# The last MLP product of a two-layer trunk: where the right half of the second token half is accumulated in PSUM

## The chip, the cores and the metric

The kernel runs on one core of a Trainium2 chip. The metric is the device time of one execution in microseconds. Before the change three runs gave 563.83, 564.20 and 564.38 us, so the median is 564.2 us.

## The reference

Two layers work on 256 tokens of width 1024. Each is a token mixer (block attention in layer 0, dilated windows in layer 1), a LayerNorm, an MLP and a second LayerNorm. Only the MLP and the norm behind it matter here:

```python
def layer_norm(x, g, b):
    mu = mean(x); var = mean((x - mu) ** 2)
    return (x - mu) * rsqrt(var + 1e-5) * g + b

def sq_relu_mlp(x, w_in, w_out):               # w_in 1024 x 4096, w_out 4096 x 1024
    return jnp.square(jax.nn.relu(x @ w_in)) @ w_out

h = layer_norm(DEEPNORM_ALPHA * h + sq_relu_mlp(h, w_in, w_out), ln_mlp_g, ln_mlp_b)
```

The norm at the end of layer 1 gives the output.

## The kernel before, in words

**Precision.** Every operand is kept as two rounded parts, hi and lo, and every product is three: hi by hi, hi by lo and lo by hi. All of these are recorded by one helper, `mm` (line 353), so nearly every TensorE row carries this line, and the tiles' names tell products apart. A weight tile of 128 x 1024 is loaded into `raw` by SyncE's queue; ScalarE rounds it to `whi` (line 344) and VectorE subtracts to get `wlo` (line 349).

**The MLP (`Mlp.rest`, from line 877).** The 4096 hidden columns are cut into eight chunks of 512. Chunk 0 is done ahead, in another form. For each chunk from 1 to 7 the first product (`mm_wstat_wide`, line 472) forms four tiles of 128 hidden columns by 256 tokens, each in a PSUM bank with the tag `tp`: per tile eight matmuls of 512 columns (hi weights by hi and lo inputs side by side) and eight of 256 (lo weights). `relu_sq_T` (line 833) takes a bank out: ScalarE copies one half (line 838), VectorE adds the other (line 535), squares (line 542), ScalarE and VectorE split the result into `ahi` and `alo`. One chunk behind, `do_out` (line 886) issues the second product with the four slices of 128 hidden columns of the chunk before, called k-tiles here; there are 32, numbered 0 to 31.

**The second product (`mm_rows`, line 515).** The 256 tokens are two halves of 128 (m = 0 and m = 1), and the outputs are 1024 columns wide. A *piece* is a PSUM bank with the first column and the number of columns that it collects. For each k-tile and each token half, every piece gets three matmuls. `new_acc` (line 814) lists the pieces: normally two of 512 columns for each token half, in four banks of the tag `acc`. In the last MLP (`last=True`, layer 1) the right half of m = 1 is two pieces of 256 columns: one in its `acc` bank and one in a bank taken from the four `tp` banks. That `tp` bank is held from k-tile 0 to the end of the kernel, so three are left for the first product's tiles. Per k-tile m = 1 then costs 3 matmuls of 512 columns and 6 of 256, where m = 0 costs 6 of 512.

**The tail (`out_and_ln`, line 820).** `TAIL` (line 30) says how many of the last k-tiles are kept back for each sub-layer; its last entry, 8, is for the last MLP. With them the pieces are finished one by one, and not k-tile by k-tile, so that VectorE can take out the first pieces while TensorE works on the next.

**The norm (`ln_half`, line 765).** For each piece VectorE computes `ALPHA * z + acc` into the token tile (lines 776 and 542) and statistics by `bn_stats` (line 779); `step` is the smallest piece, so 512 for m = 0 and 256 for m = 1 of the last MLP. Then `bn_aggr` (line 782), an addition (line 783), a power on GpSimd (line 785), two multiplications per half (line 542) and the output DMAs (line 798).

**The order of instructions.** The lists above are not the order on the engines. Each operation is recorded with an estimated cost, and a planner (`Plan.order`, line 159) simulates the engines with these costs, gives each operation a due time and picks the most urgent ready one. Buffers of a tag are given out in the order of their making; the tag `tp` alone may be taken out of turn if a bank is spare. So a change in costs or in banks held can change the order on every engine.

Of the kernel before, what the change touches and what calls it, by code (L numbers as in the profile page):

```python
# [10 lines left out]
ALU = mybir.AluOpType  # L11

P = 128
S = 256
# [8 lines left out]
ALPHA = (2.0 * DEPTH) ** 0.25  # L23
# [3 lines left out]
BIG = 3.0e38  # L27
NCH = DFF // 512
NX = (1, 1)
TAIL = (6, 4, 6, 8)  # L30
NSLOT = 10

GROUPS = ((0, 1, 2, 3),)
# [251 lines left out]
def tile_trunk(  # L285
# [37 lines left out]
    def mk(shape, dt, tag, bufs, space=None):  # L323
        uid[0] += 1
        return plan.buf(Bufs(space or sb, bufs), shape, dt, tag, bufs, f"{tag}_{uid[0]}")

    def psum(tag):
        return mk([P, 512], F32, tag, 4, ps_pool)
# [7 lines left out]
    def dve(n, aps=0, fast=False):  # L336
        return n / (1920 if fast else 960) + 0.07 + 0.06 * aps
# [14 lines left out]
    def mm(out_ap, lhsT, rhs, start, stop):  # L352
        nc.tensor.matmul(out_ap, lhsT, rhs, start=start, stop=stop)  # L353
# [160 lines left out]

    def mm_rows(pieces, item, m):
        (ahi, alo, j), w, pos, total = item
        first, last = pos == 0, pos == total - 1
        t = slice(m * P, (m + 1) * P)

        def go():  # L520
            a, b = ahi.t[:, j, t], alo.t[:, j, t]
            for acc, c0, n in pieces:
                mm(acc.t[:, :n], a, w.hi.t[:, c0 : c0 + n], first, False)
                mm(acc.t[:, :n], a, w.lo.t[:, c0 : c0 + n], False, False)
            for acc, c0, n in pieces:
                mm(acc.t[:, :n], b, w.hi.t[:, c0 : c0 + n], False, last)

        op(
            "PE", 3 * sum(n / 2400 + 0.0135 for _, _, n in pieces), go,
            [(w.hi, 0), (w.lo, 0), (ahi, (j, m)), (alo, (j, m))], [acc for acc, _, _ in pieces],  # L530
        )

    def tt(n, out_ap, a, b, alu, r, w, eng="DVE", extra=0.0):
        if eng == "DVE":
            op("DVE", dve(n) + extra, lambda: nc.vector.tensor_tensor(out_ap(), a(), b(), op=alu), r, w)  # L535
        else:
            op("POOL", n / 480 + 0.17, lambda: nc.gpsimd.tensor_tensor(out_ap(), a(), b(), op=alu), r, w)

    def stt(n, aps, dst, a, s, b, o0, o1, r, w):
        op(  # L540
            "DVE", dve(n, aps),
            lambda: nc.vector.scalar_tensor_tensor(dst(), a(), s(), b(), op0=o0, op1=o1), r, w,  # L542
        )
# [221 lines left out]
    def ln_half(pieces, m, gb, last, ahead):  # L765
        g, b = gb
        z = xtok[m]
        step = min(n for _, _, n in pieces)
        st = mk([P, 4, 6], F32, "bst", 2)
        mv = mk([P, 2], F32, "mv", 3)  # L770
        rs = mk([P, 2], F32, "rstd", 3)
        prev = []
        ns = D // step
        for acc, c0, n in pieces:
            c = slice(c0, c0 + n)
            stt(n, 0, lambda c=c: z.t[:, c], lambda c=c: z.t[:, c], lambda: ALPHA, lambda acc=acc, n=n: acc.t[:, :n],
                ALU.mult, ALU.add, [(z, c0 // 512), acc] + prev, [(z, c0 // 512)])
            for i in range(c0 // step, (c0 + n) // step):
                op("DVE", dve(step), lambda i=i: nc.vector.bn_stats(st.t[:, i, :], z.t[:, i * step : (i + 1) * step]),  # L779
                   [(z, c0 // 512)], [(st, i)])  # L780
                prev = [(st, i)]
        op("DVE", 0.24, lambda: nc.vector.bn_aggr(mv.t, st.t[:, :ns, :]), [st], [mv])
        op("DVE", 0.07, lambda: nc.vector.tensor_scalar(rs.t[:, 0:1], mv.t[:, 1:2], EPS, None, op0=ALU.add),
           [mv], [(rs, 0)])
        op("POOL", 0.98, lambda: nc.gpsimd.tensor_tensor(rs.t[:, 1:2], rs.t[:, 0:1], expo.t, op=ALU.pow),
           [(rs, 0), expo], [(rs, 1)])
        for n in range(2):
            c = slice(n * 512, (n + 1) * 512)
            stt(512, 1, lambda c=c: z.t[:, c], lambda c=c: z.t[:, c], lambda: mv.t[:, 0:1], lambda c=c: g.t[:, c],
                ALU.subtract, ALU.mult, [(z, n), mv, g], [(z, n)])  # L790
            split_last = last and m == 1 and n == 1
            for i, w in enumerate((256, 256) if split_last else (512,)):
                cw = slice(c.start + 256 * i, c.start + 256 * i + w)
                key = (z, ("part", i) if split_last else n)
                stt(w, 1, lambda cw=cw: z.t[:, cw], lambda cw=cw: z.t[:, cw], lambda: rs.t[:, 1:2],
                    lambda cw=cw: b.t[:, cw], ALU.mult, ALU.add, [(z, n), (rs, 1), b], [key])
                if last:
                    op("SP", ISSUE, lambda cw=cw: nc.sync.dma_start(out[m * P : (m + 1) * P, cw], z.t[:, cw]),
                       [key], (), early=8.0 - 8.0 * m - n)
            if not last:  # L800
                ps = psum("tp")
                transposes(
                    ps, [(j * P, lambda k=n * 4 + j: z.t[:, k * P : (k + 1) * P]) for j in range(4)], [(z, n)],
                    ahead,
                )
                t = slice(m * P, (m + 1) * P)
                keys = [(n * 4 + j, m) for j in range(4)]
                split(
                    512, lambda ps=ps: ps.t.rearrange("p (j s) -> p j s", j=4), lambda n=n: xs[n].t[:, :, 0, t],
                    lambda n=n: xs[n].t[:, :, 1, t], [ps], [(xs[n], (0, *k)) for k in keys],  # L810
                    [(xs[n], (1, *k)) for k in keys],
                )

    def new_acc(last=False):
        acc = [[(psum("acc"), n * 512, 512) for n in range(2)] for _ in range(2)]
        if last:
            acc[1] = [acc[1][0], (acc[1][1][0], 512, 256), (psum("tp"), 768, 256)]
        return acc

    def out_and_ln(acc, items, ntail, gb, last, between):  # L820
        k = len(items) - ntail
        for item in items[:k]:
            for m in range(2):
                mm_rows(acc[m], item, m)
        for m in range(2):
            for piece in acc[m]:
                for item in items[k:]:
                    mm_rows([piece], item, m)
            if m == 1 and between:
                between()  # L830
            ln_half(acc[m], m, gb, last, AHEAD["turn"][m])
# [27 lines left out]
    class Mlp:  # L859
# [17 lines left out]
        def rest(self, between):  # L877
            i, nx, chunks = self.i, self.nx, self.chunks
            self.half(1)
            acc = new_acc(self.last)  # L880
            nkt = DFF // P
            ntail = TAIL[2 * i + 1]
            pend = list(range(nx))
            tail = []

            def do_out(c):
                for j in range(4):
                    pos = c * 4 + j
                    item = ((*chunks[c], j), load_w(wout[i][pos]), pos, nkt)
                    if nkt - pos <= ntail:  # L890
                        tail.append(item)
                    else:
                        for m in range(2):
                            mm_rows(acc[m], item, m)

            for c in range(nx, NCH):
                if c == 4:
                    gb = load_gb(2 * i + 1)
                    if i == 0:
                        ropes.append(const(rope1, [P, 2, S], "ropet"))  # L900
                        late["m1"] = const(mask1, [P, 2, 512], "m1")
                chunks[c] = act_tiles()
                for js in GROUPS:
                    tiles = [(psum("tp"), load_w(win[i][c * 4 + j])) for j in js]
                    mm_wstat_wide(tiles)
                    for (ps, w), j in zip(tiles, js):
                        relu_sq_T(ps, *chunks[c], j)
                pend.append(c)
                while len(pend) > 1:
                    do_out(pend.pop(0))  # L910
            while pend:
                do_out(pend.pop(0))
            out_and_ln(acc, tail, len(tail), gb, self.last, between)

    def layer0(between):
# [84 lines left out]
        items = [((*attn[j // 4], j % 4), load_w(wo0[j]), j, 8) for j in range(8)]  # L1000
        out_and_ln(new_acc(), items, TAIL[0], (late["g"], late["b"]), False, between)

# [16 lines left out]
    def layer1(between):  # L1019
# [72 lines left out]
        items = [((*attn[j // 3], j % 3), load_w(wo1[j]), j, 6) for j in range(6)]  # L1092
        out_and_ln(new_acc(), items, TAIL[2], gb, False, between)

# [116 lines left out]
```

## Time and profile before

| what | value |
|---|---|
| median of three runs | 564.2 us (563.83 to 564.38) |
| the profiled execution's own time | 565.42 us |
| its span in the trace | 563.5 us |
| TensorE matmul (PE) busy in the span | 554.2 us |
| VectorE (DVE) busy | 413.3 us |
| ScalarE (ACT) busy | 300.5 us |
| mean granted TensorE clock | 0.996 |

The span runs from the first to the last event of the trace; the execution's own time is 1.92 us longer. A matmul row gives its start and its modelled duration. Since matmuls are pipelined, the time that one costs in a row of them is the distance from its start to the next start, not its duration. The chain of work that ended last lists, in order of time, stretches of one engine, line and output tile with their number of matmuls; a few per cent of the records may be missing, and what a stretch is called (`acc` or `tp`) is the tag of the bank that is written. Layer 0's MLP lies at about 130 to 293 us, layer 1's at about 376 to 563.5 us.

### The profile page before, as it was taken

The page shows a single profiled execution, that of the slowest core. Times are in us where ns is not written, and L with a number is a line of the kernel's source. Part 1 is how long each engine was busy: PE and PEld are TensorE (multiplying, and loading weights), DVE is VectorE, ACT ScalarE, POOL GpSimd, SP SyncE. Part 2 cuts the span into 40 slices and gives each one's busy share as a digit, 9 for nine tenths or more (in the row PEclk, how much of TensorE's full clock was granted, in tenths as well). Part 3 has the DMA queues.
Part 4 walks back from the last instruction along what each step waited for, and adds up shares of the span by engine and source line. Part 5 has one row for each costly group of instructions (what it writes and reads, how often), then busy time and mean ns, then how long its engine had stood idle before and what let it go on. Part 6 is the DMA issues. An engine that isn't in the chain of part 4 may idle for free.

```text
span 563.5 us, 8714 instructions
## 1 busy us (share of the span) xinstructions
PE 554.2 (98%) x3310; PEld 477.1 (85%) x3310; DVE 413.3 (73%) x727; ACT 300.5 (53%) x491; POOL 8.3 (1%) x13
## 2 busy tenths in 40 slices
PE   8999999999999999999999999999999999999994
PEld 8988877888888888888888889888888888888884
DVE  5799899897764854855879899789856647648554
ACT  5558889168455455455534566546545554544400
POOL 0000000000000000000000000010000000000000
PEclk9999999999999999999999999999999999999998
DMA  8996155638884755656437534516876547553001
GB/s 302 342 360 217 47 187 177 235 106 298 275 274 150 255 158 185 222 158 217 131 130 245 182 120 166 195 66 202 314 238 218 186 153 223 186 188 112 1 1 74
DMA packets 30137, 105.62 MB, mean 187 GB/s; under 512 B 3344, under 2 KB 3984, under 8 KB 30096
## 3 DMA queue, kind: packets, MB, share of 16 engines
q1 hardware_dynamic: 30096, 105.07, 55.4%
q8 instruction: 26, 0.43, 0.3%
q14 instruction: 15, 0.12, 0.1%
HBM read 104.01 MB, written 1.05 MB: 186 GB/s over the span
## 4 chain that ended last, share of the span: by engine, by line
PE 95%; ACT 2%; DVE 1%; DMA 1%; issue 0%; DVEq 0%; SPq 0%; ACTq 0%
PE acc L353 55%; PE tp L353 38%; PE tp L658 3%; ACT whi L344 1%; DMA raw<-in_xw_dram 1%; DVE tok L542 0%; DVE ta L535 0%; ACT pt L666 0%; DVE sc L634 0%; ACT ta L563 0%; ACT q0hi L344 0%; ACT q1hi L344 0%; DVE bst L779 0%; DVEq L1205 0%; SPq L340 0%
## 5 line engine op out<-in xcount | busy, mean ns | idle before, releaser
L349 DVE TENSOR_TENSOR wlo<-raw,whi 128x1024 fp32r<-128x1024 f32 (+3 forms) x186 | 218.4, 1191 | 102.5 <-PE tp L353 50.0
L344 ACT ACTIVATE whi<-raw 128x1024 fp32r<-128x1024 f32 (+1 forms) x184 | 189.1, 1043 | 141.0 <-PE tp L353 69.4
L353 PE MATMUL acc<-whi,ahi 128*128 128x512 f32 (+1 forms) x312 | 119.1, 382 | 0.0
L353 PE MATMUL acc<-wlo,ahi 128*128 128x512 f32 (+1 forms) x312 | 117.4, 380 | 0.0
L353 PE MATMUL tp<-xs,whi 128*128 128x512 f32 x448 | 106.0, 390 | 0.0
L353 PE MATMUL acc<-whi,alo 128*128 128x512 f32 (+1 forms) x312 | 100.8, 379 | 0.0
L353 PEld LDWEIGHTS tp<-xs,whi 128*128 128x128 f32 x448 | 83.5, 188 | 17.0
L353 PEld LDWEIGHTS acc<-whi,ahi 128*128 128x128 f32 x312 | 58.7, 188 | 10.7 <-issue 0.3
L353 PEld LDWEIGHTS acc<-wlo,ahi 128*128 128x128 f32 x312 | 58.8, 188 | 10.4
L353 PEld LDWEIGHTS acc<-whi,alo 128*128 128x128 f32 x312 | 57.1, 188 | 10.3
L353 PE MATMUL acc<-xs,whi 128*128 128x512 f32 (+1 forms) x272 | 57.7, 363 | 0.6 <-ACT whi L344 0.6
L353 PEld LDWEIGHTS tp<-xs,wlo 128*128 128x128 f32 x448 | 56.5, 191 | 1.6
L353 PE MATMUL tp<-xs,wlo 128*128 128x256 f32 x448 | 57.0, 283 | 0.0
L353 PEld LDWEIGHTS acc<-xs,whi 128*128 128x128 f32 x272 | 46.0, 198 | 8.1 <-ACT whi L344 1.0
L344 ACT ACTIVATE ahi<-ta 128x256 fp32r<-128x256 f32 x56 | 22.6, 413 | 29.0 <-DVE ta L542 28.8
L838 ACT ACTIVATE ta<-tp 128x256 f32<-128x256 f32 x56 | 21.2, 378 | 21.3 <-PE tp L353 21.3
L535 DVE TENSOR_TENSOR ta<-tp,ta 128x256 f32<-128x256 f32 x56 | 23.4, 417 | 11.2 <-ACT ta L838 11.0
L353 PE MATMUL acc<-xs,wlo 128*128 128x256 f32 x224 | 31.1, 287 | 0.0
L353 PEld LDWEIGHTS acc<-xs,wlo 128*128 128x128 f32 x224 | 29.7, 195 | 1.1 <-issue 0.2
L353 PE MATMUL acc<-whi,xs 128*128 128x512 f32 (+1 forms) x112 | 29.0, 367 | 0.0
L353 PE MATMUL tp<-whi,xs 128*128 128x512 f32 x80 | 25.0, 396 | 0.0
L542 DVE SCALAR_TENSOR_TENSOR ta<-ta 128x256 f32<-128x256 f32 x56 | 23.7, 424 | 1.6
(97 smaller groups left out, 503.5 us busy)
## 6 DMA issues: line engine op xcount, KB each, us to landing
raw<-in_win_dram SPq DMA_DIRECT2D x64, 512.0 KB, 4.3
raw<-in_wout_dram SPq DMA_DIRECT2D x64, 512.0 KB, 4.3
raw<-in_wqk_dram SPq DMA_DIRECT2D x22, 512.0 KB, 5.5
raw<-in_wo_dram SPq DMA_DIRECT2D x14, 512.0 KB, 3.9
raw<-in_wv_dram SPq DMA_DIRECT2D x8, 512.0 KB, 6.1
g<-in_lng_dram SPq DMA_DIRECT2D x4, 512.0 KB, 5.6
b<-in_lnb_dram SPq DMA_DIRECT2D x4, 512.0 KB, 7.2
raw<-in_wv1a_dram SPq DMA_DIRECT2D x4, 512.0 KB, 4.4
```

The costliest lines, as they stand in the source:

```text
L344: op("ACT", act(n, sbuf=sbuf), lambda: nc.scalar.activation(hi(), src(), AF.Copy), r, whi)
L349: lambda: nc.vector.tensor_tensor(lo(), src(), f32(hi()), op=ALU.subtract), list(r) + list(whi), wlo,
L353: nc.tensor.matmul(out_ap, lhsT, rhs, start=start, stop=stop)
L535: op("DVE", dve(n) + extra, lambda: nc.vector.tensor_tensor(out_ap(), a(), b(), op=alu), r, w)
L542: lambda: nc.vector.scalar_tensor_tensor(dst(), a(), s(), b(), op0=o0, op1=o1), r, w,
L658: nc.tensor.transpose(ps.t[:, c : c + P], src(), ident.t)
L838: op("ACT", act(S), lambda: nc.scalar.activation(u(), ps.t[:, S:], AF.Copy), [ps], uk)
```

## The change

In the last MLP the right half of m = 1 is collected in one `acc` bank with 512 columns, for all k-tiles that are not in the tail. The tail has 6 k-tiles and not 8. In the tail alone, the right half is split: its left 256 columns go on in the `acc` bank, and the six products of its right 256 columns go to a fresh `tp` bank, which is made only there. So the last 256 columns are the sum of two banks. `ln_half` takes the whole `acc` bank with one 512-column operation, takes the statistics of its first 256 columns, then adds the `tp` bank by a plain addition and takes the statistics of the last 256.

```diff
-TAIL = (6, 4, 6, 8)
+TAIL = (6, 4, 6, 6)
...
     def mm_rows(pieces, item, m):
         (ahi, alo, j), w, pos, total = item
-        first, last = pos == 0, pos == total - 1
+        last = pos == total - 1
...
-            for acc, c0, n in pieces:
-                mm(acc.t[:, :n], a, w.hi.t[:, c0 : c0 + n], first, False)
+            for acc, c0, n, begin in pieces:
+                mm(acc.t[:, :n], a, w.hi.t[:, c0 : c0 + n], pos == begin, False)
                 mm(acc.t[:, :n], a, w.lo.t[:, c0 : c0 + n], False, False)
...
     def ln_half(pieces, m, gb, last, ahead):
-        step = min(n for _, _, n in pieces)
+        step = S if last and m == 1 else 512
...
-        for acc, c0, n in pieces:
+        for acc, c0, n, begin in pieces:
             c = slice(c0, c0 + n)
-            stt(n, 0, lambda c=c: z.t[:, c], lambda c=c: z.t[:, c], lambda: ALPHA, lambda acc=acc, n=n: acc.t[:, :n],
-                ALU.mult, ALU.add, [(z, c0 // 512), acc] + prev, [(z, c0 // 512)])
-            for i in range(c0 // step, (c0 + n) // step):
+            if begin:
+                tt(n, lambda c=c: z.t[:, c], lambda c=c: z.t[:, c], lambda acc=acc, n=n: acc.t[:, :n], ALU.add,
+                   [(z, c0 // 512), acc] + prev, [(z, c0 // 512)])
+            else:
+                stt(n, 0, lambda c=c: z.t[:, c], lambda c=c: z.t[:, c], lambda: ALPHA, lambda acc=acc, n=n: acc.t[:, :n],
+                    ALU.mult, ALU.add, [(z, c0 // 512), acc] + prev, [(z, c0 // 512)])
+
+            for i in range(c0 // step, min([c0 + n] + [p[1] for p in pieces if p[3] > begin]) // step):
...
-    def new_acc(last=False):
-        acc = [[(psum("acc"), n * 512, 512) for n in range(2)] for _ in range(2)]
-        if last:
-            acc[1] = [acc[1][0], (acc[1][1][0], 512, 256), (psum("tp"), 768, 256)]
-        return acc
+    def new_acc():
+        return [[(psum("acc"), n * 512, 512, 0) for n in range(2)] for _ in range(2)]
...
         for m in range(2):
-            for piece in acc[m]:
+            pieces = acc[m]
+            if last and m == 1:
+
+                bank, c0 = acc[m][1][:2]
+                pieces = [acc[m][0], (bank, c0, S, 0), (psum("tp"), c0 + S, S, items[k][2])]
+                acc[m] = acc[m] + pieces[2:]
+            for piece in pieces:
                 for item in items[k:]:
                     mm_rows([piece], item, m)
```

In the built program the change moves instructions on TensorE, VectorE and ScalarE, in layer 1's MLP alone; SyncE's queue has the same transfers in the same order. In that MLP the order on TensorE becomes that of layer 0's MLP: all four tiles of a chunk's first product (four times the hi matmuls, then four times the lo ones), then the four k-tiles of the chunk before, each with 12 matmuls of 512 columns.

More of the change, by code (lines that the diff above doesn't have):

```diff
@@ L521, in go @@
             a, b = ahi.t[:, j, t], alo.t[:, j, t]
-            for acc, c0, n in pieces:
-                mm(acc.t[:, :n], a, w.hi.t[:, c0 : c0 + n], first, False)
+            for acc, c0, n, begin in pieces:
+                mm(acc.t[:, :n], a, w.hi.t[:, c0 : c0 + n], pos == begin, False)
                 mm(acc.t[:, :n], a, w.lo.t[:, c0 : c0 + n], False, False)
-            for acc, c0, n in pieces:
+            for acc, c0, n, _ in pieces:
                 mm(acc.t[:, :n], b, w.hi.t[:, c0 : c0 + n], False, last)
         op(
-            "PE", 3 * sum(n / 2400 + 0.0135 for _, _, n in pieces), go,
-            [(w.hi, 0), (w.lo, 0), (ahi, (j, m)), (alo, (j, m))], [acc for acc, _, _ in pieces],
+            "PE", 3 * sum(p[2] / 2400 + 0.0135 for p in pieces), go,
+            [(w.hi, 0), (w.lo, 0), (ahi, (j, m)), (alo, (j, m))], [p[0] for p in pieces],
         )
@@ L773, in ln_half @@
         ns = D // step
-        for acc, c0, n in pieces:
+        for acc, c0, n, begin in pieces:
             c = slice(c0, c0 + n)
-            stt(n, 0, lambda c=c: z.t[:, c], lambda c=c: z.t[:, c], lambda: ALPHA, lambda acc=acc, n=n: acc.t[:, :n],
-                ALU.mult, ALU.add, [(z, c0 // 512), acc] + prev, [(z, c0 // 512)])
-            for i in range(c0 // step, (c0 + n) // step):
+            if begin:
[5 more added lines that the diff above has]
+            for i in range(c0 // step, min([c0 + n] + [p[1] for p in pieces if p[3] > begin]) // step):
                 op("DVE", dve(step), lambda i=i: nc.vector.bn_stats(st.t[:, i, :], z.t[:, i * step : (i + 1) * step]),
@@ L879, in rest @@
             self.half(1)
-            acc = new_acc(self.last)
+            acc = new_acc()
             nkt = DFF // P
```

## The prediction

> **What bounds the kernel now.** I read the page first: busy times, the slices with the granted clock, and the chain of work that ended last.
>
> ```profile
> PE 554.2 (98%) x3310; PEld 477.1 (85%) x3310; DVE 413.3 (73%) x727; ACT 300.5 (53%) x491; POOL 8.3 (1%) x13
> PEclk9999999999999999999999999999999999999998
> PE 95%; ACT 2%; DVE 1%; DMA 1%; issue 0%; DVEq 0%; SPq 0%; ACTq 0%
> ```
>
> TensorE is busy for 98% of the span and owns 95% of the chain. A busy PE need not be an efficient PE, so the question for each stage is what distance its matmuls keep. The page's average cannot say that, so the next view is the chain in order of time. Layer 0's MLP and layer 1's do the same arithmetic, but layer 0 has the two plain 512-column pieces for both token halves, which is what the change gives layer 1 outside its tail. The first fence is layer 0, the second layer 1, each over five whole chunks (start, length, engine and what is written, matmuls).
>
> ```profile
> 151.01 11.09 PE tp L353 x64
> 162.10 10.91 PE acc L353 x48
> 173.01 11.09 PE tp L353 x64
> ...
> 260.98 11.09 PE tp L353 x64
> ```
>
> ```profile
> 411.51 8.46 PE tp L353 x49
> 419.97 1.39 PE acc L353 x6
> 421.36 2.77 PE tp L353 x16
> ...
> 433.76 8.46 PE tp L353 x49
> ...
> 522.78 11.27 PE tp L353 x65
> 534.05 16.75 PE acc L353 x78
> ```
>
> Five chunks of layer 0 take 260.98 - 151.01 = 109.97 us, so 21.994 each; five of layer 1 take 522.78 - 411.51 = 111.27, so 22.254 each. Layer 1 pays 0.260 us more per chunk. Is that waiting, or the matmuls themselves? The table by stretch answers (PE, PEld, DVE, ACT and POOL busy with counts, clock, DMA share, GB/s):
>
> ```profile
> 151.01:173.01 22.00, 22.00 (x114) 18.86 (x113) 13.73 (x20) 11.40 (x16) 0.00 (x0) 1.00 0.84 275
> 411.51:433.76 22.25, 22.25 (x127) 19.45 (x126) 13.86 (x20) 11.13 (x16) 0.00 (x0) 1.00 0.72 240
> ```
>
> PE is busy for the whole length of each, at a granted clock of 1.00, while VectorE has 13.9 us of work in 22 and the DMA engines are below full. So both MLPs are bound by the distance between matmuls. At the end the bound changes: VectorE's norm hangs behind the last matmul.
>
> ```profile
> 554.80 0.28 PE L353 MATMUL acc<-whi,alo 128*128 128x256 f32 x1
> 555.12 0.42 DVE L542 SCALAR_TENSOR_TENSOR tok<-tok,acc 128x256 f32<-128x256 f32 x1 [1.76 <-PE acc L353]
> ...
> 555.88 0.28 PE L353 MATMUL tp<-whi,alo 128*128 128x256 f32 x1
> 556.19 0.42 DVE L542 SCALAR_TENSOR_TENSOR tok<-tok,tp 128x256 f32<-128x256 f32 x1 [0.19 <-PE tp L353]
> 556.65 0.43 DVE L779 BATCH_NORM_STATS2 bst<-tok 128x6 f32<-128x256 f32 x1
> 557.11 0.26 DVE L782 BATCH_NORM_AGGREGATE mv<-bst 128x2 f32<-128x24 f32 x1
> ```
>
> From the last matmul's start at 555.88 to the span's end at 563.5 are 7.6 us that no matmul fills.
>
> **The change, part by part.**
>
> *(a) Fewer, wider matmuls outside the tail.* Before, 24 of 32 k-tiles lie outside the tail, and each has three pairs of 256-column matmuls in m = 1 where the change has three of 512: 72 matmuls go, no column goes. They lie in six chunk periods, 1 to 6 (one chunk's k-tiles behind the next one's first product). In the built program the order on TensorE in these periods is, matmul for matmul, that of layer 0, and VectorE and ScalarE run layer 0's sequence too. So I price it by the measured difference of periods: 6 x 0.260 = **1.56 us less**. This step rests on an analogy, since no run of before has layer 1 in this form, so I bound it. A lower end: if only the 256-column matmuls' own distance counts, an item of layer 1 shows what it is.
>
> ```profile
> 427.44 0.28 PE L353 MATMUL tp<-whi,ahi 128*128 128x256 f32 x1
> 427.56 0.28 PE L353 MATMUL tp<-wlo,ahi 128*128 128x256 f32 x1
> ...
> 550.04 0.28 PE L353 MATMUL acc<-wlo,ahi 128*128 128x256 f32 x1
> 550.15 0.28 PE L353 MATMUL acc<-whi,alo 128*128 128x256 f32 x1
> ```
>
> Two of them cost 0.24 us at the common distance of 0.12, and 0.22 to 0.23 at the shortest, 0.11 to 0.12; one of 512 costs 10.91 / 48 = 0.2273. The common distance gives 72 x 0.0127 = 0.91, the shortest nothing at all. The rest of the 1.56 is the 512-column matmuls around them, which also come further apart in layer 1. The upper end is 1.6, the rounding of the periods. I take 1.56, since the period contains all of it and the analogy is exact in order, shapes and clock.
>
> At this place the Trainium skill speaks against the change. "TensorE: Matmul & The Clock Gate", section "Wait — 56ns, not 53.3ns?", gives a matmul's distance as its columns at 2.4 GHz plus about 2.5 ns. By that rule each removed matmul would save 2.5 ns, an estimate of 0.2 us for all. The trace does not agree: 512 columns keep 227 ns here and 256 keep 120, against the rule's 216 and 109. A lead of some 13 ns per pair stands where the rule has 2.5.
>
> *(b) The tail.* Before, the tail's eight k-tiles start when the last chunk's first product ends, at 522.78 + 11.09 = 533.87, and cost 72 x 0.2273 (six per k-tile in m = 0, three in m = 1) + 48 x 0.12 = 22.13 us, which gives 556.00; the trace has the last start at 555.88. After, k-tiles 24 and 25 are plain (24 matmuls of 512), then six remain in the tail: (24 + 36 + 18) x 0.2273 + 36 x 0.12 = 22.05. **0.08 us less.** Six more matmuls go, so 78 in all.
>
> *(c) One bank and not two is taken out at the end.* This adds work on VectorE behind the matmuls: the `acc` bank's operation grows from 256 to 512 columns. The left half's rows show the price of that form:
>
> ```profile
> 551.89 0.69 DVE L542 SCALAR_TENSOR_TENSOR tok<-tok,acc 128x512 f32<-128x512 f32 x1 [2.40 <-PE acc L353]
> 552.61 0.75 DVE L779 BATCH_NORM_STATS2 bst<-tok 128x6 f32<-128x256 f32 x2
> ```
>
> In the built order 12 matmuls of `tp` follow the last one of `acc`, 12 x 0.12 = 1.44 us. VectorE starts 0.32 after that `acc` matmul's start (554.80 to 555.12), is at the next operation 0.72 later (551.89 to 552.61) and past the statistics 0.46 later (556.65 to 557.11): free at +1.50. The `tp` bank is ready at 1.44 + 0.31 (555.88 to 556.19) = +1.75. So 0.25 us are to spare and the cost is **0**; without that cover it would cost at most 0.72 + 0.46 = 1.18.
>
> *(d) The plain addition for the last 256 columns.* It reads a PSUM bank and the token tile, as before. The group of line 535 with the same shape has a mean of 417 ns, the operation that it replaces 0.42 us: **0**.
>
> ```profile
> L535 DVE TENSOR_TENSOR ta<-tp,ta 128x256 f32<-128x256 f32 x56 | 23.4, 417 | 11.2 <-ACT ta L838 11.0
> ```
>
> *(e) The shorter tail gives m = 0's norm less cover.* It ran from 544.99 to 549.49:
>
> ```profile
> 544.99 0.69 DVE L542 SCALAR_TENSOR_TENSOR tok<-tok,acc 128x512 f32<-128x512 f32 x1 [3.35 <-PE acc L353]
> ...
> 548.08 1.41 DVE L542 SCALAR_TENSOR_TENSOR tok<-tok,rstd,b 128x512 f32<-128x512 f32 x2
> ```
>
> These 4.50 us now stand against 18 x 0.2273 + 3 x 0.12 = 4.45 before m = 1's left half is ready, so VectorE may start that 0.05 late. The right half's `acc` bank comes 21 x 0.12 = 2.52 later, and the left half needs 0.72 + 0.75 = 1.47: about 1.0 is left. m = 0's output DMAs are issued some 3.5 us before the last matmul and m = 1's some 3.5 behind it, as many as before and in the same order. **0**.
>
> *(f) The `tp` bank that comes free.* The fourth tile of each chunk no longer waits for a turn. PE is busy through these stretches already, so nothing is gained beyond (a), and the weights that it wants earlier are split long before in both layers.
>
> Sum: 1.56 + 0.08 = 1.64 us less. Against the profiled execution (565.42, of which the span is 563.5) that gives a span of 561.86 and an execution of 563.78; the median shown is 1.22 below that execution, so it goes from 564.2 to **562.6**. 0.2% of 564.2, about what a measurement of this kernel can tell from no change, is 1.13 us: faster ends at 563.07, slower begins at 565.33.
>
> **Rivals.**
>
> *The removed matmuls were nearly free.* If the longer distance of the 512-column matmuls in layer 1 comes from something that stays, only the pairs count, at most 78 x 0.0127 = 0.99 and at the shortest distance next to nothing: 563.2 to 564.2, middle 563.7. For it: PE's cost is a distance, and no column goes. Against it: layer 0's periods, with the same first product, are 0.260 shorter throughout. The 2.5 ns rule of the Trainium skill ("TensorE: Matmul & The Clock Gate") would come out here as well, by estimate at 564.0. Chance 0.10.
>
> *VectorE becomes the bound behind the last matmul.* If its 512-column operation ends later than the `tp` bank by the full 1.18 of (c), the time is 563.8. Against it stand the 0.25 to spare; it decides once `acc` ends less than 1.19 us before `tp`. Chance 0.04.
>
> *The last chunk feeds the tail too late, and the kernel is slower.* With two more plain k-tiles first, PE wants the last chunk's first slice 30 matmuls after its first product, at +6.8 us, the others at +8.2, +9.5 and +10.9. If ScalarE and VectorE deliver later, PE stops, and each microsecond is one at the end; it takes 1.64 + 1.13 = 2.8 us of stop to read slower. Layer 0's slices came at these times, its first product ending at 162.10:
>
> ```profile
> 163.52 0.42 DVE L349 TENSOR_TENSOR alo<-ta,ahi 128x256 fp32r<-128x256 f32 x1
> ...
> 170.31 0.42 DVE L349 TENSOR_TENSOR alo<-ta,ahi 128x256 fp32r<-128x256 f32 x1
> ```
>
> That is +1.8 for the first and +8.6 for the last, with four weight splits between them where the last chunk has two. So 2.3 us are to spare, and VectorE would have to be 5 us later than in layer 0: time 565.4 or more, chance 0.02.
>
> **How the numbers follow.** The forecast has 0.84, the rivals 0.10, 0.04 and 0.02. The forecast's own spread is that of the runs (0.55 between three) around 562.6, so about 562.0 to 563.1. The range reaches into the nearly-free rival, 561.9 to 563.5. Faster by over 0.2%: the forecast and a little of the first rival, 0.85; within: 0.12; slower: 0.03.
>
> **What would show it.** Right: chunk periods of 21.99 us in layer 1, with 64 `tp` and 48 `acc` matmuls in turn; a tail of 22.05 us; the last `tp` addition starting about 0.3 us behind the last matmul's start, VectorE idle just before it; the same 7.6 us behind that. Wrong: periods above 22.1, or idle time on PE between the last first product and the tail, or the addition released by VectorE itself and not by TensorE.

## The result, and the profile after

Fifteen runs of the changed kernel have a median of 562.55 us (561.57 to 565.70), fifteen of the kernel before one of 564.20 (563.74 to 566.76). The ratio is 0.997, with a 95% interval of 0.9958 to 0.9983: faster by 0.3%, and a ratio of 1, no change, lies outside the interval. The forecast was 562.6.

The page of the changed kernel, its busy times and the chain by engine:

```profile
PE 552.0 (98%) x3232; PEld 472.9 (84%) x3232; DVE 412.8 (74%) x727; ACT 301.8 (54%) x491; POOL 8.3 (1%) x13
PEclk9999999999999999999999999999999999999998
PE 95%; ACT 2%; DVE 1%; DMA 1%; issue 0%; DVEq 0%; SPq 0%; ACTq 0%
```

3310 matmuls have become 3232, 78 fewer, as the prediction counted. VectorE has the same number of instructions. The shares tell nothing of the gain; the chain in order of time does. These are layer 1's chunks now (start, length, engine and what is written, matmuls):

```profile
390.98 9.10 PE tp L353 x55
400.08 10.91 PE acc L353 x48
410.99 11.09 PE tp L353 x64
422.07 10.91 PE acc L353 x48
432.98 11.09 PE tp L353 x64
...
520.95 11.09 PE tp L353 x64
532.04 19.15 PE acc L353 x90
```

Five chunks from 410.99 to 520.95 take 109.96 us, 21.99 each, where they took 111.27. They are layer 0's chunks to the hundredth: 64 matmuls in 11.09, then 48 in 10.91. And PE is as busy as before in each of them, which is why a busy share cannot show such a gain (columns as in the prediction):

```profile
410.83:432.82 21.99, 21.99 (x114) 18.86 (x113) 13.74 (x20) 11.40 (x16) 0.00 (x0) 1.00 0.70 239
```

The end of the kernel, in the order of time, TensorE's and VectorE's rows together:

```profile
552.34 0.28 PE L353 MATMUL acc<-whi,alo 128*128 128x256 f32 x1
...
553.78 0.28 PE L353 MATMUL tp<-whi,alo 128*128 128x256 f32 x1
```

```profile
548.79 1.41 DVE L542 SCALAR_TENSOR_TENSOR tok<-tok,rstd,b 128x512 f32<-128x512 f32 x2
550.15 0.69 DVE L542 SCALAR_TENSOR_TENSOR tok<-tok,acc 128x512 f32<-128x512 f32 x1
...
552.66 0.69 DVE L542 SCALAR_TENSOR_TENSOR tok<-tok,acc 128x512 f32<-128x512 f32 x1 [1.04 <-PE acc L353]
553.39 0.43 DVE L784 BATCH_NORM_STATS2 bst<-tok 128x6 f32<-128x256 f32 x1
554.10 0.42 DVE L535 TENSOR_TENSOR tok<-tok,tp 128x256 f32<-128x256 f32 x1 [0.28 <-PE tp L353]
554.55 0.43 DVE L784 BATCH_NORM_STATS2 bst<-tok 128x6 f32<-128x256 f32 x1
555.02 0.26 DVE L787 BATCH_NORM_AGGREGATE mv<-bst 128x2 f32<-128x24 f32 x1
```

The last row that decides is the addition at 554.10: VectorE was idle for 0.28 us before it and was released by TensorE. So VectorE is not the bound there.

**Where the time went.** The two profiled spans differ by 563.5 - 561.4 = 2.1 us, more than the medians do. Three events split it: the start of chunk 1's first product, the end of the last matmul by the chain, and the end of the span. The first two stand in these rows of the chain, of the kernel before (the matmuls end at 555.08 + 1.09 = 556.17) and of the changed one (chunk 1 at 390.98 above, the matmuls' end at 552.62 + 1.45 = 554.07):

```profile
391.39 6.33 PE tp L353 x39
...
555.08 1.09 PE tp L353 x9
```

```profile
552.62 1.45 PE tp L353 x12
```

| stretch | before | after | difference |
|---|---|---|---|
| start of the span to chunk 1 of layer 1's MLP | 391.39 | 390.98 | -0.41 |
| chunk 1 to the end of the last matmul | 164.78 | 163.09 | -1.69 |
| from there to the end of the span | 7.33 | 7.33 | 0.00 |

The first stretch holds nothing that the change touches. Its difference is there by 30 us already, in the opening loads (the first token projection is over at 30.02 before and at 29.61 after), and it goes up and down by more than that in the runs below. The change is the second row, -1.69 us.

### The profile page after: what moved, and what is told of

Same layout as the page of the kernel before. It is cut to its first block, busy times and chain, and to the rows that moved or that the text cites. A ratio compares the mean times of both kernels' runs of the same rounds, so it can differ in the third digit from the quotient of the medians.

```text
span 561.4 us, 8567 instructions
## 1 busy us (share of the span) xinstructions
PE 552.0 (98%) x3232; PEld 472.9 (84%) x3232; DVE 412.8 (74%) x727; ACT 301.8 (54%) x491; POOL 8.3 (1%) x13
## 4 chain that ended last, share of the span: by engine, by line
PE 95%; ACT 2%; DVE 1%; DMA 1%; issue 0%; DVEq 0%; SPq 0%; ACTq 0%
PE acc L353 57%; PE tp L353 36%; PE tp L658 3%; ACT whi L344 1%; DMA raw<-in_xw_dram 1%; DVE ta L535 0%; DVE tok L542 0%; ACT pt L666 0%; DVE sc L634 0%; ACT ta L563 0%; ACT q0hi L344 0%; ACT q1hi L344 0%; DVE bst L784 0%; DVE tok L535 0%; DVEq L1213 0%
## 5 line engine op out<-in xcount | busy, mean ns | idle before, releaser
L353 PE MATMUL acc<-whi,ahi 128*128 128x512 f32 (+1 forms) x312 | 121.8, 390 | 0.0
L353 PE MATMUL acc<-wlo,ahi 128*128 128x512 f32 (+1 forms) x312 | 121.2, 389 | 0.0
L353 PE MATMUL tp<-xs,whi 128*128 128x512 f32 x448 | 104.7, 390 | 0.0
L353 PE MATMUL acc<-whi,alo 128*128 128x512 f32 (+1 forms) x312 | 102.8, 388 | 0.0
L353 PEld LDWEIGHTS acc<-whi,alo 128*128 128x128 f32 x312 | 58.6, 188 | 12.1
```

## The experiments

The theory is the prediction's: the price is paid per matmul, so cutting a 512-column product in two costs time that PE shows as busy. The first rival puts it on the bank: while one `tp` bank is held, a chunk's four tiles cannot be done together, and the order on TensorE is another. The runs are compared by chunk period (the distance from one chunk's first product to the next one's), and by the stretch from chunk 1 to the last matmul, because the opening varies from run to run. The stretch repeats well: 164.78 and 164.79 us in the two kernels of the table with the old pieces. The kernel before was timed again beside each group of runs (medians 564.49 of 29 and 564.82 of 13), and the ratios below are to these runs.

| kernel | chunk period | cuts per chunk | chunk 1 to last matmul | last matmul to end |
|---|---|---|---|---|
| before | 22.25 | 12 | 164.78 | 7.33 |
| after | 21.99 | 0 | 163.09 | 7.33 |
| cut in one bank (e1) | 22.26 | 12 | 164.74 | 7.38 |
| bank held, nothing cut (e2) | 22.01 | 0 | 163.39 | 7.37 |
| cut 384 + 128 (e3) | 22.90 | 12 | 168.74 | 7.33 |
| both right halves cut (e4) | 22.31 | 24 | 165.13 | 7.29 |
| m = 1 cut on both sides (e9) | 22.39 | 24 | 165.58 | 7.30 |
| tail of 4 (e6) | 21.99 | 0 | 163.00 | 7.57 |
| no split in the tail (e7) | 21.99 | 0 | 162.84 | 7.82 |
| before, tail of 6 (e8) | 22.25 | 12 | 164.79 | 7.36 |

### The cut without the held bank

```diff
...
+        if cut and pos:
+            acc, c0, n, begin = pieces[-1]
+            parts = parts[:-1] + [(acc, c0 + o, x, begin, o) for o, x in zip((0, cut[0]), cut)]
...
```

> The changed kernel, but outside the tail the right half of m = 1 is cut into two matmuls of 256 columns again, for k-tiles 1 to 25, both into the one acc bank. The order on every engine stays that of the changed kernel and no tp bank is held. If the distance of the cut matmuls was the price (0.260 / 12 = 0.0217 us per cut), 75 cuts cost 1.63 us: chunk periods 22.25 us, time 564.2. If the held bank and the order that it forced were the price: periods 21.99, time 562.6.

The chain of this kernel:

```profile
411.74 11.11 PE tp L354 x64
422.85 11.15 PE acc L354 x60
434.00 11.11 PE tp L354 x64
```

The order is the changed kernel's (64 and 60 in turn, no bank held), and the period is 22.26, 0.27 above the changed kernel's: the whole of the old price is back. The theory holds; the rival's 21.99 does not. The timed runs have a median of 565.64 (563.78 to 566.68) and a ratio to before of 1.0015 (1.0004 to 1.0027), above the 564.2 expected. The profile does not show the excess: the stretch from chunk 1 to the last matmul is 164.74 against 164.78 before. Where these runs' remainder lies stays open.

### The held bank without the cut

```diff
...
+            if self.last:
+                late["tp"] = psum("tp")
...
+                        if self.last and pos == 0:
+                            hold(late["tp"], item)
```

> The changed kernel, but the tp bank of the last 256 columns is taken at the first k-tile (by one extra matmul of 256 columns, overwritten later) and held to the end, so each chunk's first product has three banks and its fourth tile comes behind the first matmuls of a k-tile, as before the change. All matmuls stay 512 wide outside the tail. If the cut is the price: periods 21.99 us and 562.7. If the held bank is: periods 22.25 and 564.2.

The chain of this kernel:

```profile
411.81 8.31 PE tp L353 x48
420.12 1.39 PE acc L353 x6
421.51 2.77 PE tp L353 x16
424.27 9.55 PE acc L353 x42
433.82 8.31 PE tp L353 x48
```

Here is the old order, three tiles, six matmuls of the second product, the fourth tile. Its period is 22.01, so the held bank and the order cost 0.02 us per chunk and the cut the other 0.24; alone, in e1, the cut costs 0.27, so the two parts do not add up to the hundredth. The time is 563.07 (ratio 0.9977, 0.9966 to 0.9989).

### Another place for the cut

```diff
-CUT = (None, (256, 256))
+CUT = (None, (384, 128))
```

> As e1, but each cut is 384 + 128 columns and not 256 + 256. If a matmul costs its columns plus a fixed 14 ns, the place of the cut is of no account: periods about 22.2 us, 564.2. If a matmul has a least distance, of about 0.12 us, that 256 columns just reach, then 128 columns pay far more than their share: 0.174 + 0.118 against 0.227, so 0.065 per cut, periods 22.77 and 567.4.

The chain and some matmuls of the timeline:

```profile
410.90 11.18 PE tp L354 x64
422.08 11.72 PE acc L354 x60
433.80 11.18 PE tp L354 x64
```

```profile
427.05 0.22 PE L354 MATMUL acc<-whi,ahi 128*128 128x128 f32 x1
427.11 0.27 PE L354 MATMUL acc<-wlo,ahi 128*128 128x128 f32 x1
427.22 0.68 PE L354 MATMUL acc<-whi,alo 128*128 128x512 f32 x3
427.74 0.45 PE L354 MATMUL acc<-whi,ahi 128*128 128x512 f32 x1
428.03 0.40 PE L354 MATMUL acc<-wlo,ahi 128*128 128x512 f32 x1
```

The period is 22.90, so a cut costs 0.91 / 12 = 0.076 us here and 0.022 in e1, with the same columns and the same number of matmuls. A fixed cost alone falls. The least distance came near in size, with 0.065 expected, but not in form: by the rows one 128-column matmul is followed after 0.06 already, the next only after 0.11, and a wide one behind two of them takes 0.29 (427.74 to 428.03) and not 0.227. (The row of three at 427.22 takes together matmuls of 512, 384 and 128 columns and shows the first one's shape.) The time is 568.71 (ratio 1.0075, 1.0062 to 1.0088); 567.4 was expected.

### Twice as many cuts, spread and together

```diff
-CUT = (None, (256, 256))
+CUT = ((256, 256), (256, 256))
```

> As e1, but the right halves of both token halves are cut into 256 + 256: 150 cuts. If the price is per cut and adds up: periods 21.99 + 24 x 0.0217 = 22.51 us, 565.8. If most of the price in e1 is at the change from wide to narrow and back, less than double of e1's extra: under 22.4.

```diff
-            acc, c0, n, begin = pieces[-1]
-            parts = parts[:-1] + [(acc, c0 + o, x, begin, o) for o, x in zip((0, cut[0]), cut)]
+            parts = [(acc, c0 + o, x, begin, o) for acc, c0, n, begin in pieces for o, x in zip((0, cut[0]), cut)]
```

> As e1, but both pieces of m = 1 are cut into 256 + 256, so 24 cuts per chunk as in the run with both right halves cut, where the extra was 0.32 us per chunk. If the price is a fixed cost per matmul of some 13 ns: 0.32 again, periods 22.31. If an all-wide m = 0 that follows a narrow m = 1 pays another 0.025 per k-tile, as the rows of e1 look: 0.42, periods 22.41.

The first chain is of the kernel with both right halves cut, the second of that with all of m = 1 cut:

```profile
410.34 11.11 PE tp L354 x64
421.45 11.20 PE acc L354 x72
432.65 11.11 PE tp L354 x64
```

```profile
411.39 11.11 PE tp L354 x64
422.50 11.28 PE acc L354 x72
433.78 11.11 PE tp L354 x64
```

Both have 24 cuts per chunk. The first pays 0.32 us for them, not the 0.52 that e1's price would give, so its second expectation (under 22.4) came out; the second pays 0.40, near the 0.42 of its second expectation. Per cut that is 13 ns, 17 ns, and 22 ns in e1: there is no fixed price. The timed runs have a median of 565.03 (ratio 1.0013, 0.9998 to 1.0028; 565.8 was the first expectation) and, of the second kernel, a single time of 565.96.

The rows show that wide matmuls pay too, in both kernels. First the one with both right halves cut, then that with all of m = 1 cut:

```profile
426.89 0.40 PE L354 MATMUL acc<-whi,ahi 128*128 128x512 f32 x1
427.12 0.40 PE L354 MATMUL acc<-wlo,ahi 128*128 128x512 f32 x1
427.36 0.28 PE L354 MATMUL acc<-whi,ahi 128*128 128x256 f32 x1
```

```profile
427.98 0.40 PE L354 MATMUL acc<-whi,ahi 128*128 128x512 f32 x1
...
429.36 0.28 PE L354 MATMUL acc<-whi,ahi 128*128 128x256 f32 x1
```

The two wide ones of the first take 0.47 us where 0.45 would be two of 0.2273; the six of the second take 1.38 where 1.36 would be six. The traces hold the starts in nanoseconds, and with them the price of a k-tile can be split (two middle k-tiles of a chunk, mean of five chunks; the changed kernel has 2720 ns per k-tile, 226.7 per matmul):

| kernel | extra on the 256-column matmuls, ns | extra on the 512-column ones, ns | sum, ns |
|---|---|---|---|
| right half of m = 1 cut (e1) | 31 | 36 | 67 |
| both right halves cut (e4) | 32 | 48 | 80 |
| all of m = 1 cut (e9) | 73 | 27 | 100 |

Four k-tiles of these sums are the 0.27, 0.32 and 0.40 us per chunk. In e9 ten of the twelve narrow matmuls in a row keep 120 ns each; in e4, where two or four narrow ones stand between wide ones, the narrow ones keep 113 to 119 and the wide ones 233 to 236. So the price of before was of two kinds, in about equal parts: narrow matmuls cost more than half of a wide one, and the wide ones behind them come further apart. Why the wide ones pay is open; nothing tried takes it apart. Each matmul loads its own weights (3310 loads for 3310 matmuls before), so a cut adds a load with each matmul, and no run separates the two.

### The tail

> The kernel before with 6 k-tiles in the tail and nothing else changed: the same matmuls, the cuts stay everywhere. If the gain is the wide matmuls': no change, 564.2 to 564.4, chunk periods 22.25, tail about the same. If the shorter tail has a part of the gain by itself: up to 0.5 us less.

The edit is `TAIL` alone, in the kernel before. Ten runs have a median of 565.57 (ratio to before 1.0006, 0.9989 to 1.0023), and chunk 1 to the last matmul is 164.79 against 164.78. The shorter tail by itself brings nothing, as its first expectation said.

> The changed kernel with 4 k-tiles in the tail and not 6. TensorE: 6 cuts fewer, 0.08 us less. VectorE: m = 0's norm (4.50 us) has only 18 x 0.2273 = 4.09 before m = 1's left half, so it starts that 0.4 late, is behind the left half at about +6.0 where the acc bank is ready at +5.5, and the tp addition starts about 0.2 us after its bank is ready. Theory of prediction part (c) and (e): the cover runs out here, the addition starts about 0.5 us behind the last matmul's start and not 0.31, and waits for VectorE; total within 0.15 of the change. Rival: cover is not what decides, the addition still starts 0.31 behind.

The edit is `TAIL = (6, 4, 6, 4)` in the changed kernel. VectorE at the end:

```profile
550.71 0.68 DVE L542 SCALAR_TENSOR_TENSOR tok<-tok,acc 128x512 f32<-128x512 f32 x1
551.43 0.43 DVE L784 BATCH_NORM_STATS2 bst<-tok 128x6 f32<-128x256 f32 x1
551.81 0.69 DVE L542 SCALAR_TENSOR_TENSOR tok<-tok,acc 128x512 f32<-128x512 f32 x1
552.53 0.43 DVE L784 BATCH_NORM_STATS2 bst<-tok 128x6 f32<-128x256 f32 x1
553.25 0.42 DVE L535 TENSOR_TENSOR tok<-tok,tp 128x256 f32<-128x256 f32 x1 [0.29 <-PE tp L353]
553.59 0.74 DVE L784 BATCH_NORM_STATS2 bst<-tok 128x6 f32<-128x256 f32 x2
```

The size came out (163.00 and 7.57, together 0.15 us more than the change), the way did not. The cover does run out: the left half waits for m = 0's norm until 550.71, with no idle time before it. But the addition was expected 0.5 us behind the last matmul's start and waiting for VectorE, and it is on time: 0.32 us behind that start (552.93) and released by TensorE, which was the rival's number. In the planner's order one of the left half's two statistics stands behind the addition, and so 0.2 us are paid after it (from the addition's start to that of the operation that brings the statistics together, line 787, it is 1.12 us in place of the changed kernel's 0.92). Its single time is 562.68 us.

> The changed kernel without the split in the tail: the right half stays one piece of 512 columns, statistics over 512. TensorE: 18 cuts fewer at about 0.0135, tail 21.8 us. VectorE behind the last matmul: 0.72 + 0.72 in place of 0.46 + 0.46, so 0.52 more there. Sum about 0.28 us slower than the change; if the split's matmuls cost more than VectorE's wait, it is faster.

```diff
-            if last and m == 1:
+            if False:
...
-        step = S if last and m == 1 else 512
+        step = 512
```

```profile
530.98 21.80 PE acc L353 x96
...
552.80 0.70 DVE tok L542
...
553.52 0.70 DVE bst L784
```

The tail is 21.80 us as expected, and 7.82 follow: 0.25 us gained by TensorE, 0.49 lost behind it, 0.24 slower in sum, where 0.28 was expected. The split in the tail is worth that, less than the timed runs can tell. Its one run took 562.51 us, with an opening that ended 1.04 us earlier than the changed kernel's (389.94 against 390.98).

## Why the prediction was right

**(a) Wider matmuls.** Forecast 0.260 per chunk period, measured 22.254 - 21.992 = 0.262. From chunk 1 to the start of the tail (534.05 and 532.04) it is 142.66 against 141.06, 1.60 us, where 1.56 was the sum. Pricing by layer 0's periods, and not by the pairs alone, was the step that mattered. Pairs alone would have given 0.91, and the rows of e1 show why that is too small: more than half of the price stands on the wide matmuls behind the narrow ones (36 of 67 ns). The prediction had named this part, and put 0.65 of its 1.56 us there. That the cut is the cause, and not the bank, is shown by e1 and e2.

**(b) The tail.** Forecast 22.13 to 22.05; the chain gives 22.12 (534.05 to 556.17) and 22.03 (532.04 to 554.07). The tail of before begins at 534.05 and not at the 533.87 worked out, since the chain's stretch of 65 holds a matmul of the k-tile before; the difference of the two tails does not hang on it.

**(c) VectorE behind the last matmul.** Forecast 0.25 us to spare, measured 0.28, and the addition starts 0.32 behind the last matmul's start at 553.78. The `acc` bank's last matmul stands at 552.34, 1.44 ahead, as worked out.

**(d), (f)** cost nothing, as forecast: the addition takes 0.42, and e2 puts the freed bank at 0.02 per chunk.

**(e) Less cover for m = 0's norm.** The left half is taken out at 550.15, straight behind that norm and 0.43 behind its own last matmul's start (549.72), the distance that it has in the kernel before, where VectorE waited for it (551.46 to 551.89). So it is not late, where 0.05 was forecast: the norm took 4.45 us (545.70 to 550.15) and not 4.50. The 1.04 us of idle time before the right half's operation would have taken it up. With two k-tiles fewer (e6) the cover is gone, and 0.2 us appear.

The sum was 1.64 and the trace has 1.69. That the median of 562.55 is within 0.05 us of the forecast is in part luck: the base was the median of three runs, and the kernel before had medians of 564.20, 564.49 and 564.82 in its three groups of runs. The rival that the removed matmuls were nearly free is out by the chunk periods. The rule of the Trainium skill that it had beside it ("TensorE: Matmul & The Clock Gate", section "Wait — 56ns, not 53.3ns?"), some 2.5 ns per matmul, does not agree with the 13 to 22 ns per cut of e4, e9 and e1; the measurement decides, for matmuls that each load their weights. That VectorE becomes the bound, or that the last chunk feeds the tail too late, is out by the rows of the end: PE is busy without a gap to 554.07, and the addition is released by TensorE.

## What to carry to other kernels

When TensorE is busy all the time, look at the distance from matmul to matmul: cutting a product to free an engine at the end is paid in every iteration, so cut only in the iterations that the end needs. If another stage of the same kernel already runs the form that a change will give, its period prices the change better than a sum of single rows, since a narrow matmul also slows the wide ones behind it. Compare two kernels by the stretch that the change touches, not by their spans.

## What the runs showed of the hardware

A cut's price depends on its place and on what is around it: in all 22 ns for 256 + 256 in e1, 17 in e9, 13 in e4, and 76 for 384 + 128. Wide matmuls behind narrow ones need several matmuls to come back to their distance: in e1 237, 235, 232 and 231 ns, and then 227. The opening varies more than this change is worth: chunk 1 of layer 1's MLP starts between 389.94 and 392.15 us in ten profiles, though nothing ahead of it differs between the kernels. The first load has a part in it: on the chain of e7, where chunk 1 starts first, it took 2.92 us, and 4.54 in the kernel before with a tail of 6, where chunk 1 starts last. It is not all: in e4 that load took longer than in the changed kernel (3.58 and 3.37), and chunk 1 starts 0.90 us earlier (390.08 and 390.98). What else varies stays open.
